# Modulation steps, casts and one transpose issued at other places of a two-layer hybrid block

## The chip, the core and the metric

One Trainium2 chip, of which the program uses one core. The metric is the device time of one execution in microseconds (us). The engines are TensorE (PE: matmuls, and PEld: its weight loads), VectorE (DVE), ScalarE (ACT), GpSimd (POOL) and SyncE (SP, which here only issues transfers). Each works through its own instructions in the order in which the program issues them, and waits on semaphores for the others.

## The reference

Two layers run over 256 latent tokens (x) and 256 context tokens (ctx), 1024 wide, in fp32. Each layer has an FFN, a mixer of three head groups (neighbourhood attention, spatial gating, retention), and a second FFN. Nine modulation vectors of 1024 (shift, scale and gate for each of the three parts) come from c for latent tokens and from c_ctx for context tokens. After the second mixer only latent tokens go on.

```python
mod_x = (jax.nn.silu(c) @ ada_w[layer] + ada_b[layer]).reshape(b, N_MOD, 1, d)
mod_c = (jax.nn.silu(c_ctx) @ ada_w[layer] + ada_b[layer]).reshape(1, N_MOD, 1, d)
x = ffn_branch(x, mod_x, 0, ...)      # h + 0.5 * gate * swiglu(rms(h) * (1 + scale) + shift)
ctx = ffn_branch(ctx, mod_c, 0, ...)
yx, yc = hybrid_mixer(...)
x = x + mod_x[:, 5] * yx
x = ffn_branch(x, mod_x, 6, ...)
if not last:
    ctx = ctx + mod_c[:, 5] * yc
    ctx = ffn_branch(ctx, mod_c, 6, ...)
return x
```

## The kernel before, in words

Tokens lie along the free axis: xT holds 8 tiles of 128 features by 512 tokens (256 latent, 256 context). Every large product is made of three matmuls on split operands: each fp32 operand is a high part (a cast to fp32r) and a low part (the rest), and high by high, high by low and low by high are added up in PSUM (L204, L206 to L208; L212 for the other layout).

**Weights.** `Stream` (L64) brings the weights in 128x1024 chunks in a fixed order. A chunk is loaded by a transfer on SP's queue into one of three `wr` buffers (L79), cast by ScalarE into `wh` (L89), and VectorE subtracts to give `wl` (L100); four buffers each. `take` hands out the next chunk and prefetches up to three more; `high_to` issues casts alone. So the low part of a chunk stands in VectorE's queue about one output tile before TensorE needs it.

**An FFN** (L625) runs in two halves. In each, `up` makes 11 gate and 11 up outputs (16 products of 512 tokens for each pair; L675 gates, L679 casts the result, L682 gives its low part), then `down` makes 8 output tiles (11 products each) and `residual` (L441) adds each to xT. In the second half the normalization of what follows is prepared: ScalarE squares each new tile (L337), VectorE adds up (L341). Where both token streams go on, the last two output tiles are done stream by stream (`split_tail`), and the first chunks of the next phase are split between them (`todo`, `hand_over`: code 1k is a cast up to chunk k, 2k a cast and low part up to chunk k). There are four FFNs: (0,0), (0,1), (1,0), (1,1). In (0,1) and (1,0) most up products use seven products for eight (`Seven`), and in (1,1) only latent tokens are left.

**The planner.** Work that is not tied to a product waits in two lists. `bg` is a list of steps; `pump` (L185) is called after every product of three matmuls, and adds `pace[0]` for 512 columns (half of it for 256); each whole one issues a step. `due` holds functions that `later` puts there with a delay in the same counts. `drain_bg` issues all that is left.

**Modulation.** `ada_steps` (L264) makes the modulation vectors on VectorE: each block of 128 outputs is one 512 KB tile `aw`, loaded by a transfer (L282), and one step per token stream multiplies it with the vector and sums (L290, whose output goes to `junk` or in place to `aw`); after 8 blocks a closing step adds the bias (L295). Vectors 5 to 8 of layer 1 need only the latent stream: one step on a tile instead of two. All 112 steps of layer 1 are spread over the FFNs by `ADA1`: for each FFN the counts in its first and second half. In (0,0) the list is 112 steps of layer 0 and then those of layer 1, at `APACE`, with five `aw` buffers on SP's queue. In (0,1) and (1,0) the steps run in the down phases, in the first half with two `aw` buffers (which the up phases use too) and in the second with four, both on POOL's queue. In (1,1) they run in the first up phase.

**The end of the last mixer.** `yt` (L1510) transposes the retention output of one pair of heads (yR, made on POOL at L1302 and L1304), ScalarE writes its high part (L1515), VectorE its low part (L1516). `proj` adds the output projection up in the order of `KORD`: features 0 to 2 are attention, 3 and 4 gating (`sg_gate`, L1379; split at L1507 and L1508), 5 to 7 retention. In layer 1 two output tiles (`NM`) are begun together while these come in.

Of the kernel before, what the change touches and what calls it, by code (L numbers as in the profile page):

```python
# [20 lines left out]
KT = D // 128  # L21
# [16 lines left out]

DIRECT = {(0, 1): (5, 0), (1, 0): (5, 0)}

ADA1 = {(0, 0): (40, 0), (0, 1): (16, 16), (1, 0): (16, 16), (1, 1): (8, 0)}

STAT, OS, FS, SPR = 3, 3.5, 2, 12

# [9 lines left out]
SUMS = 0.65  # L54
GPACE = (0.4, 0.55)
OPACE = (0.8, 0.8)
APACE = 0.345
NPACE = (0.95, 1.0)
RPACE = (1.2, 1.4)

# [74 lines left out]
def tile_hybrid_dit(ctx: ExitStack, tc: tile.TileContext, t_x, t_c, t_cb, t_ada0, t_ada, t_adab, t_nw, t_w1, t_w2,  # L135
# [12 lines left out]
    def mm_bank(name="mm"):  # L148
        return bank("mm", 4, name)
# [48 lines left out]
    def drain_bg(n=None):  # L198
        while bg and (n is None or n > 0):
            bg.pop(0)()  # L200
            if n is not None:
                n -= 1
# [16 lines left out]
    with tc.manual_schedule():  # L219
# [219 lines left out]
        def residual(l, i, m, ps, c0, streams):  # L439
            for s in streams:  # L440
                V.scalar_tensor_tensor(out=xT[:, m, s * T:s * T + T], in0=ps[:, s * T - c0:s * T - c0 + T],  # L441
                                       scalar=mod[l][:, 24 * i + 16 + m, s:s + 1], in1=xT[:, m, s * T:s * T + T],
                                       op0=ALU.mult, op1=ALU.add)
# [181 lines left out]
        def ffn(l, f, lead, norms, steps=None, tail=None):  # L625
# [7 lines left out]
            with ExitStack() as es:  # L633
# [21 lines left out]
                for half in range(2):  # L655
# [114 lines left out]
                    def down(m, wa, wb, a, b, ps):  # L770
                        for kt in range(JH):
                            w, c = (wa, kt) if kt < 6 else (wb, kt - 6)
                            product(ps[:, a:b], w, 128 * c, aTh, aTl, (slice(None), kt, slice(a, b)),
                                    kt == 0, kt == JH - 1)
# [15 lines left out]
                    for m in range(KT - 2 if split_tail else KT):  # L790
                        a, b = 0, T * len(streams)
                        wa, wb = ws.take(), ws.take(AHEAD - 1)
                        ps = mm_bank("d")
                        if ahead and m == KT - 3:
                            drain_bg()
                            seven.load(JH)
                            seven.load(JH + 1)
                            seven.add(JH)
                            seven.add(JH + 1)
                        down(m, wa, wb, a, b, ps)  # L800
                        if ahead and m >= KT - 2:
                            for s in seven.prepare(JH)[slice(0, 4) if m == KT - 2 else slice(4, 7)]:
                                s()
                        residual(l, i, m, ps, 0, streams)
                        if half == 1:
                            for s in streams:
                                if s in norms:
                                    norms[s].add(m)
                            if tail:
                                tail(m)  # L810
                    if split_tail:
                        w = [(ws.take(3), ws.take(2)), (ws.take(1), ws.take(0))]
                        for s in streams:
                            for m in (KT - 2, KT - 1):
                                ps = mm_bank("d")
                                down(m, *w[m - KT + 2], s * T, s * T + T, ps)
                                residual(l, i, m, ps, 0, (s,))
                                norms[s].add(m)
                                if s and m < KT - 1:
                                    flush_due()  # L820
                                    for f in todo(norms, steps[0]):
                                        f()
                            if s == 0:
                                later(FS, norms[0].stats)
                                later(FS + 2, norms[0].begin)
                                drain_bg()
                            else:
                                hand_over(norms, steps[1])
# [37 lines left out]
        def mixer(l, norms):  # L866
            last = l == L - 1
            ctx_out = not last
            with ExitStack() as es:
# [631 lines left out]


                yh, yl = hTh, hTl
                KORD = (0, 1, 2, 5, 6, 7, 3, 4)

                def split(src, dst):
                    S.copy(out=yh[dst], in_=src)  # L1507
# [10 lines left out]

                def proj(m, w, ps, a, b, kts=KORD):
                    for kt in kts:  # L1520
                        hh, hl = (na["oT"][:, 0], na["oT"][:, 1]) if kt < 3 else (yh, yl)
                        product(ps[:, a:b], w, 128 * kt, hh, hl, (slice(None), kt, slice(a, b)),
                                kt == KORD[0], kt == KORD[-1])

# [6 lines left out]
                for m in range(nm):  # L1531
                    if m < 3:
                        yt(m + 5)
                    proj(m, w[m], ps[m], 0, n, KORD[0:3])
                for m in range(nm, 3):
                    yt(m + 5)
                for kt in KORD[3:6]:
                    for m in range(nm):
                        proj(m, w[m], ps[m], 0, n, (kt,))
                drain_bg()  # L1540

                def finish(m, ps, ahead=AHEAD):
                    residual(l, 1, m, ps, 0, streams)
# [6 lines left out]
                            norms[0].raw(k)  # L1550

                for m in range(nm):
                    proj(m, w[m], ps[m], 0, n, KORD[6:8])
                    finish(m, ps[m], min(m + 5 - nm, AHEAD))
                for m in range(nm, KT - 3 if ctx_out else KT):
                    w = ws.take(0)
# [290 lines left out]
```

## Time and profile before

| | |
|---|---|
| time, 3 runs | 1810.83 us median (1810.07 to 1811.4) |
| profiled execution | 1812.95 us; span of the core 1811.2 us |
| mean granted TensorE clock | 0.997 |
| PE busy | 1778.7 us (98%), 11520 matmuls |
| DVE busy | 1300.8 us (72%) |
| ACT busy | 724.8 us (40%) |
| POOL busy | 260.8 us (14%) |
| HBM read | 287.64 MB |

Times in the rows are microseconds from the start of the span. A busy share is an average over stages; which engine is waited for is read stage by stage. Matmuls are pipelined: a 512-column product is shown about 0.39 us long while the next starts 0.23 us after it, a 256-column one 0.28 us long with the next after 0.12 us.

### The profile page before, as it was taken

How to read it: one execution, taken by the hardware profiler on the slowest of the kernel's cores; microseconds unless marked ns; L12 is line 12 of the kernel's file. 1: busy time of each engine (PE TensorE's matmuls, PEld its weight loads, DVE VectorE, ACT ScalarE, POOL GpSimd, SP SyncE). 2: the span in 40 equal slices, each digit the busy share in tenths (PEclk: the TensorE clock that was granted, in tenths of full speed). 3: DMA queues.
4: the chain of work that ended last, by engine and by line, in shares of the span. 5: the costliest groups of instructions: out<-in, count | busy, mean ns of one | idle time of the engine just before them, and what ended most of it. 6: DMA issues, size and time to landing. Idle time of an engine off the chain costs nothing. (4 is left out here: it accounts for less than half of the span.)

```text
span 1811.2 us, 29366 instructions
## 1 busy us (share of the span) xinstructions
PE 1778.7 (98%) x11520; PEld 1550.2 (86%) x11520; DVE 1300.8 (72%) x2200; ACT 724.8 (40%) x1203; POOL 260.8 (14%) x307
## 2 busy tenths in 40 slices
PE   7999999999999999999999999999999999999999
PEld 5788888888668989898999898979998867899998
DVE  5789988976455566788588877776887745668665
ACT  3422222225544234452344244513542555354443
POOL 0000000002114310120222002113311104310000
PEclk9999999999999999999999999999999999999999
DMA  8656765634211122656675526567666422356654
GB/s 316 236 190 217 252 212 189 212 124 149 87 64 47 47 74 67 174 147 188 179 183 158 164 86 179 153 210 199 169 188 222 146 88 76 106 192 200 200 179 148
DMA packets 103610, 290.60 MB, mean 160 GB/s; under 512 B 12080, under 2 KB 18864, under 8 KB 103344
## 3 DMA queue, kind: packets, MB, share of 16 engines
q1 hardware_dynamic: 86192, 243.64, 41.0%
q0 software_dynamic: 17280, 45.10, 10.8%
q8 instruction: 90, 1.47, 0.3%
q14 instruction: 48, 0.39, 0.1%
HBM read 287.64 MB, written 1.05 MB: 159 GB/s over the span
## 5 line engine op out<-in xcount | busy, mean ns | idle before, releaser
L100 DVE TENSOR_TENSOR wl<-wr,wh 128x1024 fp32r<-128x1024 f32 (+2 forms) x308 | 327.0, 1087 | 112.3 <-ACT wh L89 110.9
L89 ACT CAST wh<-wr 128x1024 fp32r<-128x1024 f32 (+2 forms) x308 | 279.9, 934 | 182.2 <-PE d L207 90.5
L208 PE MATMUL d<-aTh,wl 128*128 128x512 f32 (+1 forms) x770 | 269.6, 350 | 2.0 <-DVE wl L100 2.0
L206 PE MATMUL d<-aTh,wh 128*128 128x512 f32 (+1 forms) x770 | 269.9, 351 | 1.1 <-ACT wh L89 1.1
L207 PE MATMUL d<-aTl,wh 128*128 128x512 f32 (+1 forms) x770 | 269.2, 350 | 0.0
L208 PEld LDWEIGHTS d<-aTh,wl 128*128 128x128 f32 x770 | 145.3, 189 | 24.4 <-DVE wl L100 3.2
L206 PEld LDWEIGHTS d<-aTh,wh 128*128 128x128 f32 x770 | 145.2, 189 | 22.5 <-ACT wh L89 1.3
L290 DVE CUSTOM_DVE_ANT_0 aw<-aw,cb 128x1024 f32<-128x1024 f32 x128 | 155.6, 1223 | 11.5 <-DMA aw<-in_ada_dram 8.9
L207 PEld LDWEIGHTS d<-aTl,wh 128*128 128x128 f32 x770 | 145.3, 189 | 21.1
L206 PE MATMUL g<-hTh,wh 128*128 128x512 f32 (+2 forms) x464 | 158.1, 341 | 3.0 <-ACT hTh L383 1.4
L208 PE MATMUL g<-hTh,wl 128*128 128x512 f32 (+2 forms) x464 | 156.9, 338 | 2.0 <-DVE wl L100 1.9
L207 PE MATMUL g<-hTl,wh 128*128 128x512 f32 (+2 forms) x464 | 157.1, 339 | 1.3 <-DVE hTl L366 1.1
L208 PE MATMUL u<-hTh,wl 128*128 128x512 f32 (+2 forms) x464 | 156.6, 337 | 0.4 <-DVE wl L100 0.4
L206 PE MATMUL u<-hTh,wh 128*128 128x512 f32 (+2 forms) x464 | 156.1, 336 | 0.0
L207 PE MATMUL u<-hTl,wh 128*128 128x512 f32 (+2 forms) x464 | 156.0, 336 | 0.0
L214 PE MATMUL nat<-wh,hTh 128*128 128x512 f32 (+2 forms) x384 | 136.3, 355 | 0.0
L216 PE MATMUL nat<-wh,hTl 128*128 128x512 f32 (+2 forms) x384 | 127.9, 333 | 0.4 <-DVE hTl L366 0.4
L215 PE MATMUL nat<-wl,hTh 128*128 128x512 f32 (+2 forms) x384 | 127.7, 333 | 0.0
L290 DVE CUSTOM_DVE_ANT_0 junk<-aw,cb 128x1024 f32<-128x1024 f32 x96 | 117.0, 1219 | 4.5 <-DMA aw<-in_ada_dram 4.1
L582 PE MATMUL p<-hTh,wl 128*128 128x256 f32 x408 | 116.2, 285 | 0.6
L582 PE MATMUL p<-th,wl 128*128 128x256 f32 x408 | 114.8, 281 | 0.6 <-DVE wl L551 0.5
L581 PE MATMUL p<-hTl,wh 128*128 128x256 f32 x408 | 114.6, 281 | 0.0
(262 smaller groups left out, 4044.5 us busy)
## 6 DMA issues: line engine op xcount, KB each, us to landing
wr<-in_w_dram SPq DMA_DIRECT2D x142, 512.0 KB, 4.4
aw<-in_ada_dram SPq DMA_DIRECT2D x92, 512.0 KB, 5.1
wr<-in_wi_dram SPq DMA_DIRECT2D x56, 512.0 KB, 3.6
aw<-in_ada_dram POOLq DMA_DIRECT2D x52, 512.0 KB, 4.8
wr<-in_w_dram SPq DMA_DIRECT2D x64, 384.0 KB, 3.8
wr<-in_w_dram SPq DMA_DIRECT2D x64, 320.0 KB, 3.0
q<-in_w_dram SPq DMA_DIRECT2D x68, 256.0 KB, 3.8
q<-in_w_dram POOLq DMA_DIRECT2D x68, 256.0 KB, 5.3
```

The lines of the kernel that those rows point to most:

```text
L89: self.nc.scalar.copy(out=h[:, :n], in_=self.raw[i][:, :n])
L100: self.nc.vector.tensor_tensor(out=lo[:, :n], in0=t[:, :n], in1=h[:, :n].bitcast(F32), op=ALU.subtract)
L206: PE.matmul(out=ps, lhsT=wh[:, col:col + 128], rhs=hh[rhs_sl], start=start, stop=False)
L207: PE.matmul(out=ps, lhsT=wh[:, col:col + 128], rhs=hl[rhs_sl], start=False, stop=False)
L208: PE.matmul(out=ps, lhsT=wl[:, col:col + 128], rhs=hh[rhs_sl], start=False, stop=stop)
L214: PE.matmul(out=ps, lhsT=hh[lhs_sl], rhs=wh[:, wc], start=start, stop=False)
L215: PE.matmul(out=ps, lhsT=hh[lhs_sl], rhs=wl[:, wc], start=False, stop=False)
L216: PE.matmul(out=ps, lhsT=hl[lhs_sl], rhs=wh[:, wc], start=False, stop=stop)
L290: V.tensor_tensor_reduce(out=junk, in0=t, in1=cb[:, s], scale=1.0, scalar=0.0, op0=ALU.mult, op1=ALU.add, accum_out=mod[l][:, 8 * r + b, s ...
L581: PE.matmul(out=ps, lhsT=wh[:, cw], rhs=tl, start=False, stop=False)
L582: PE.matmul(out=ps, lhsT=wl[:, cw], rhs=th, start=False, stop=n == 3)
```

## The change

Five edits. The constants: eight more steps of layer 1 in (0,0), none in (1,1), and a pace of 0.38 instead of 0.345 in (0,0). Since the steps are taken from one list in order, the four places between keep their counts (16 each) and get later vectors. In the second half of each FFN with `split_tail`, the casts of the last output tile's two chunks are issued before the residual of the sixth tile. In the last tiles' second stream, the cast and the low part of the next phase's first chunk are put into the due list at 3.1 and 4.1 counts, ahead of the residual of the seventh tile. In the last layer's mixer, the projection's order takes the gating features before the last retention pair, and that pair's transpose is issued after them.

```diff
-ADA1 = {(0, 0): (40, 0), (0, 1): (16, 16), (1, 0): (16, 16), (1, 1): (8, 0)}
+ADA1 = {(0, 0): (48, 0), (0, 1): (16, 16), (1, 0): (16, 16), (1, 1): (0, 0)}
...
-APACE = 0.345
+APACE = 0.38
...
+                        if split_tail and m == KT - 3:
+                            ws.high_to(ws.n_take + 4)
                         residual(l, i, m, ps, 0, streams)
...
                                 ps = mm_bank("d")
+                                if s and m < KT - 1:
+
+                                    for n, f in enumerate(todo(norms, (11, 21))):
+                                        later(3.1 + n, f)
                                 down(m, *w[m - KT + 2], s * T, s * T + T, ps)
...
-                KORD = (0, 1, 2, 5, 6, 7, 3, 4)
+                KORD = (0, 1, 2, 5, 6, 3, 4, 7) if last else (0, 1, 2, 5, 6, 7, 3, 4)
...
-                for m in range(nm, 3):
+                for m in range(nm, 2 if last else 3):
                     yt(m + 5)
-                for kt in KORD[3:6]:
+                for kt in KORD[3:7 if last else 6]:
                     for m in range(nm):
                         proj(m, w[m], ps[m], 0, n, (kt,))
                 drain_bg()
+                if last:
+                    yt(7)
...
                 for m in range(nm):
-                    proj(m, w[m], ps[m], 0, n, KORD[6:8])
+                    proj(m, w[m], ps[m], 0, n, KORD[7 if last else 6:])
                     finish(m, ps[m], min(m + 5 - nm, AHEAD))
```

## Rows read from the trace of the kernel before

**Rows 1.** Part 1 of the page: busy time, share, instructions.
```profile
PE 1778.7 (98%) x11520; PEld 1550.2 (86%) x11520; DVE 1300.8 (72%) x2200; ACT 724.8 (40%) x1203; POOL 260.8 (14%) x307
```
**Rows 2.** TensorE's waits, 387 to 400 us: total, times, longest (us).
```profile
PE d L206 <- ACT wh L89: 1.1, 1, 1.1
PE d L208 <- DVE wl L100: 0.5, 1, 0.5
```
**Rows 3.** Busy time, one stretch: length, PE, PEld, DVE, ACT, POOL, PEclk, DMA.
```profile
393.30:396.80 3.50, 3.50 (x19) 3.50 (x19) 2.12 (x5) 0.42 (x1) 0.00 (x0) 0.52 0.86 269
```
**Rows 4.** VectorE's groups, 57 to 387 us: busy us, mean ns, idle before.
```profile
L290 DVE CUSTOM_DVE_ANT_0 junk<-aw,cb 128x1024 f32<-128x1024 f32 x75 | 91.5, 1219 | 4.5 <-DMA aw<-in_ada_dram 4.1 <-ACT cb L1718 0.4
L290 DVE CUSTOM_DVE_ANT_0 aw<-aw,cb 128x1024 f32<-128x1024 f32 x74 | 90.5, 1223 | 2.0
...
L682 DVE TENSOR_TENSOR aTl<-sg,aTh 128x512 fp32r<-128x512 f32 x22 | 15.2, 692 | 15.1 <-ACT aTh L679 15.1
L675 DVE TENSOR_TENSOR sg<-sg,u 128x512 f32<-128x512 f32 x22 | 15.0, 681 | 3.4 <-PE u L208 3.4
...
L441 DVE SCALAR_TENSOR_TENSOR xT<-d,mod,xT 128x256 f32<-128x256 f32 x26 | 11.3, 477 | 1.7 <-PE d L208 1.7
```
**Rows 5.** Timeline, PE and DVE, 156 to 165 us: start, length, what.
```profile
156.10 0.40 PE L208 MATMUL u<-hTh,wl 128*128 128x512 f32 x1
...
160.06 0.68 DVE L675 TENSOR_TENSOR sg<-sg,u 128x512 f32<-128x512 f32 x1
...
162.16 1.69 DVE L100 TENSOR_TENSOR wl<-wr,wh 128x768 fp32r<-128x768 f32 x2
...
164.51 0.39 PE L208 MATMUL d<-aTh,wl 128*128 128x512 f32 x1
```
**Rows 6.** Timeline, PE and DVE, second half of the first FFN.
```profile
340.20 0.40 PE L208 MATMUL u<-hTh,wl 128*128 128x512 f32 x1
...
341.12 0.68 DVE L675 TENSOR_TENSOR sg<-sg,u 128x512 f32<-128x512 f32 x1
...
386.40 0.39 PE L208 MATMUL d<-aTh,wl 128*128 128x512 f32 x1
...
389.63 0.87 DVE L441 SCALAR_TENSOR_TENSOR xT<-d,mod,xT 128x256 f32<-128x256 f32 x2
```
**Rows 7.** TensorE's waits, 1048 to 1056 us.
```profile
PE g L207 <- DVE hTl L366: 0.7, 1, 0.7
PE u L208 <- DVE wl L100: 0.4, 1, 0.4
```
**Rows 8.** Timeline, POOL, DVE and PE, first down phase of the third FFN.
```profile
1198.01 0.53 POOL L282 DMA_DIRECT2D aw<-in_ada_dram  x1 [4.24 <-DVE mod L290]
...
1202.91 1.23 DVE L290 CUSTOM_DVE_ANT_0 aw<-aw,cb 128x1024 f32<-128x1024 f32 x1 [3.72 <-DMA aw<-in_ada_dram]
...
1214.91 1.23 DVE L290 CUSTOM_DVE_ANT_0 aw<-aw,cb 128x1024 f32<-128x1024 f32 x1 [2.43 <-DMA aw<-in_ada_dram]
...
1218.05 0.50 PE L208 MATMUL d<-aTh,wl 128*128 128x512 f32 x1 [0.42 <-DVE wl L100]
```
**Rows 9.** TensorE's waits, 1640 to 1690 us, last FFN.
```profile
PE g L208 <- DVE wl L100: 1.5, 2, 0.8
PE g L206 <- ACT wh L89: 1.0, 2, 0.5
PE d L208 <- DVE wl L100: 0.6, 2, 0.3
```
**Rows 10.** Timeline, DVE, PE and ACT, output projection of the last mixer.
```profile
1586.41 0.86 DVE L1516 SCALAR_TENSOR_TENSOR hTl<-yt,gnw,hTh 128x256 fp32r<-128x256 f32 x2
1587.12 0.44 PE L1513 MATMUL yt<-ident,yR 128*128 128x128 f32 x2 [2.52 <-POOL yR L1304]
...
1587.60 0.47 ACT L1515 ACTIVATE hTh<-yt,gnw 128x256 fp32r<-128x256 f32 x1 [1.40 <-PE yt L1513]
...
1588.11 0.48 DVE L1516 SCALAR_TENSOR_TENSOR hTl<-yt,gnw,hTh 128x256 fp32r<-128x256 f32 x1 [0.83 <-ACT hTh L1515]
```

## The prediction

> **What bounds the kernel now.** Read the engine shares first: TensorE is busy 98% of the span [rows 1]. So only three things can move the time: waits of TensorE, stretches at its lower clock, and new waits. Read TensorE's waits next, by stretch, and ask at each who came last. At the end of the first FFN it waits 1.1 us for a cast and 0.5 us for a low part [rows 2]; right after, the clock is at 0.52 for 3.5 us, about the lower of its two levels (1.2 against 2.4 GHz) [rows 3]. Then read the engine behind it: VectorE's groups over the first FFN, with what ended its idle time [rows 4]. Most of its time is modulation steps (149 of 1.22 us), and of its idle time only 3.4 + 1.7 us ended with TensorE's products. It is nearly full, and never the bound there: TensorE has no wait between 57 and 387 us. How much later VectorE may run before it becomes the bound is the question of this change.
>
> The profiled execution took 1812.95 us, its span 1811.2; the median of the runs shown is 1810.83. The sum below is a difference on that span and is added to the median. A wait in the rows hides 0.16 us more than it shows: a 256-column product is modelled 0.28 us long, while the next follows 0.12 us later.
>
> **Modulation steps and pace in the first FFN.** The planner counts one per three 512-column products. From the product at 156.10 to that at 164.51 [rows 5] are 36 starts, so a count is 0.70 us. The FFN has after its lead 144 counts (first half up), 88 (down), 176 (second half up), 66 (six whole down tiles). The pace goes from 0.345 to 0.38, so by the end of each stretch 5.0, 3.1, 6.2 and, until the list of 173 items runs out at count 455 (four tiles), 1.5 more steps have been issued: 15.8 x 1.22 = 19.3 us of VectorE work, with four more 512 KB loads on SP's queue (which waits for VectorE's buffers in the same order, so it brings no wait of its own).
>
> How much can hide? A step waits for no product, and the low parts of the next weights stand behind it. At 160.06 the last gating of the first half starts 3.7 us after the last up product (156.10 + 0.23); its low parts, from 162.16, are one done at about 163.0, and TensorE needs that one at 164.51 [rows 5]. So 1.5 us are spare: VectorE may be 5.2 us late there, and about as much in the down tiles; about 8 us between up tiles, which last 3.5 us longer. Stretch by stretch:
> - first half up: 3.7 + 5.0 x 1.22, less some 0.5 us of the idle time, is 9.3 us late against 5.2: some 4 us of TensorE wait;
> - down: the lag falls more slowly than before; 0.4 us, and 3.5 us late at the end;
> - second half up: before, the last gating at 341.12 is 0.7 us behind the product at 340.20 (+ 0.23) [rows 6]. Now 0.7 + 3.5 carried + 6.2 x 1.22, less the 3.4 us of idle time that ended with up products, is 8.4 late against 5 allowed: 3.4 us;
> - four down tiles: 1.5 x 1.22 more, and the growth they had before (0.7 to 2.3 us late): some 2.2 us.
> Together 10 us. After a wait as long as those 1.6 us the clock fell [rows 2, 3], and 3.5 us at half rate cost 1.7. Two such drops are likely here, but while VectorE is behind a slower TensorE mostly lets it catch up: +1. I take 11; from below nothing is charged (the lag stays in the queue), from above 14 + 3.4.
>
> **End of the first FFN.** The steps run out one and a half tiles earlier, VectorE catches up (before, the residual at 389.63 comes 3.0 us after the last product [rows 6]), and the two casts stand ahead of that residual on ScalarE. The wait goes: 1.1 + 0.5 + 2 x 0.16 = 1.9 us, and with it the 1.7 us of the clock drop: -3.6, from 0 (if the lag above is still there) to -3.7. At the other two FFN ends no product waits for these casts; cost and gain nothing, covered by the 256-column products that run meanwhile.
>
> **First cast and low part of the next phase ahead of the residual.** Three places. At 1052 us TensorE waits 0.7 + 0.4 us for a normalized tile and a low part [rows 7]; both follow the second of two low parts on VectorE, and one of these now comes a tile earlier, behind the first two scaled tiles: -1.1, from 0 to -1.4. The residual behind it is up to 1.2 us later, which the last tile's 33 products (3.9 us) hide. At the other two places at most 0.3 us either way, taken as nothing.
>
> **Modulation steps in the third FFN.** The last eight steps move forward through all FFNs. The second FFN keeps 8 loads of two steps in each half. The third FFN's first down phase had 4 loads of two steps and 8 of one (12 loads); it now has 16 of one. Its tiles have two buffers, loaded from POOL's queue. One load is issued at 1198.01, and the step on it starts at 1202.91, after 3.72 us of VectorE idle; from there to 1214.91 are four steps [rows 8], 3.0 us each. The planner issues one per 2.9 counts, 2.0 us. So each step on a tile of its own puts VectorE 1.0 us further back. Before, eight of them end in a TensorE wait of 0.42 us for a low part [rows 8]: the lag is already at its limit. Eight more add 8 x 1.0, less the first two loads that come before they are needed: 6 to 9 us, nearly all wait of TensorE since nothing is spare. What is queued behind is the residual and both low parts of every tile, then the loads of the next half, which share those buffers. I take +7; from below 0 (loads in time), from above 11. The same fall-out as above in clock: within the upper bound.
> The Trainium skill, "DMA: Bandwidth & Descriptors", section on the anatomy of a DMA on the gpsimd path, gives 2.0 us plus bytes over 436 GB/s; for 512 KB that is an estimate of 3.2 us, and with it this term would be about 1 and the sum 1814.8. The trace disagrees with it: 4.90 us from issue to step. It is the second rival.
>
> **Last FFN.** Its eight steps are gone (8 loads on POOL, one closing addition). From 1640 to 1690 us TensorE waits six times, 1.5 + 1.0 + 0.6 us [rows 9], all for casts and low parts behind those steps. With 6 x 0.16 that is 4.1 us; nothing else is late there, since the neighbouring outputs without steps have no wait. -4.0, from -3 to -4.1.
>
> **Last mixer.** The third transpose waits 2.52 us for POOL, until 1587.12 [rows 10]. Moved back, TensorE next needs the tile that VectorE finishes in the pair begun at 1586.41: the first is done at about 1586.9. So the wait is nearly as long (0.2 less), because the gating's subtraction is late too. And at its new place nothing stands between the transpose and its product: from transpose to ScalarE's copy 0.48 us, copy 0.47, VectorE's low part from 1588.11 for 0.48 [rows 10], with 0.06 to restart 1.5 us, of which transpose and first product cover 0.3: +1.2. Where the clock is low at this time anyway, part is hidden: +0.7, from -0.3 to +2.
>
> **Sum.** 11 - 3.6 - 1.1 + 7 - 4.0 + 0.7 = +10.0 us: 1820.8.
>
> **The rivals.**
> - VectorE's queue takes it all (faster): gains stay, charges don't come: -3.6 - 1.1 - 4.0 + 0.7 = -8.0, 1802.8. For it: no TensorE wait from 57 to 387 us, with VectorE 3.7 us late already. Against it: the 1.5 us to spare [rows 5] and the 0.42 us wait [rows 8]. It decides at the last gating of the first half: under 5.2 us late. 0.12.
> - The third FFN's loads come nearly in time: a step every 2.0 us needs a buffer back in 4.0, so a load in 2.7; at 3.2 a buffer turns round in 4.5, a step comes every 2.2 us, and the term is 1, not 7: +4.0, 1814.8. For it, the two loads that a buffer pair keeps under way; against it, 4.90 [rows 8]. 0.12.
> - Only the first FFN absorbs: -8.0 + 7 = -1.0, 1809.8. For it, the idle time of 15.1 us behind the copies [rows 4], if a wait for ScalarE shrinks under load; against it, those waits are in each gating's own chain. 0.09.
> - Clock drops at all four new waits cost in full, 4 x 1.7 less the 1 counted: +15.8, 1826.6. For it [rows 3]; against it, VectorE is still behind during most of these waits, and then TensorE's rate is not what counts. 0.12.
> - That the edits do nothing: the counts above come from the constants that the planner reads, so none.
>
> **How the numbers follow.** The forecast keeps 0.55; its own range is 1814 to 1828. Under 0.2% (3.6 us) this measurement can't be told from no change. Slower: 0.55 + 0.12 (clock) and most of the 0.12 of the loads, which ends at the edge: 0.73. Same: 0.09 and the rest: 0.14. Faster: 0.13. The range leaves out the absorbing case and the far ends: 1806 to 1831.
>
> **What would show it.** Right: TensorE waits for low parts at about 165 to 176 us and 350 to 362 us, VectorE's last gating of the first half 8 us late; no wait and full clock at 390 to 400; steps 3 us apart at 1180 to 1225 with a TensorE wait of 5 us or more there; no wait from 1640 to 1690; a second short wait behind the third transpose. Wrong: VectorE idle for products in the first FFN as before, or steps 2 us apart in the third.

## The result, and the profile after

The changed kernel took 1821.35 us (median of 4 runs, 1819.64 to 1825.84) against 1810.72 us (4 runs, 1810.07 to 1811.4): a ratio of 1.0055, 95% interval 1.0037 to 1.0074. It is slower by 10.6 us; the forecast was 10.0 us, 1820.8.

The profiled execution is the longest of the four (1825.84, span 1824.1), so the first question is how much of its 12.9 us of extra span is the change. Part 1 of its page answers [rows 1]: no engine has more instructions, and TensorE is busy for 5.9 us longer.

```profile
PE 1784.6 (98%) x11520; PEld 1551.5 (85%) x11520; DVE 1300.3 (71%) x2200; ACT 725.0 (40%) x1203; POOL 259.4 (14%) x303
```

Both traces hold all 11520 TensorE products, so the n-th can be laid beside the n-th. The table gives, for every kernel of this study, by how much its products fall back (+) or gain (-) against those of the kernel before between two such products (us, start of the product from the start of the span; the times in the heading are those of the kernel before).

| kernel | start-up, to 80.3 | first FFN, to 370.8 | its end, to 415.7 | mixer and second FFN, to 1021.0 | to 1181.5 | third FFN, down and up, to 1316.5 | to 1578.1 | last mixer, to 1644.3 | last FFN, to 1775.0 | to 1807.3 | sum |
|---|---|---|---|---|---|---|---|---|---|---|---|
| after | 3.47 | 7.95 | -2.21 | -0.08 | -0.21 | 8.77 | 0.00 | 1.01 | -4.71 | -0.87 | 13.11 |
| e1_old_constants | 2.77 | 0.00 | -2.27 | 3.17 | -0.21 | -1.64 | -1.61 | -0.52 | 0.01 | -0.87 | -1.17 |
| e2_constants_only | 2.03 | 8.95 | -3.11 | 0.03 | -0.20 | 8.13 | -1.63 | 0.00 | -4.71 | -0.87 | 8.62 |
| e3_pace_only | 1.87 | 8.04 | -3.67 | 1.57 | 0.37 | 0.05 | -0.02 | 0.02 | -0.06 | -0.58 | 7.60 |
| e4_two_loads | 3.04 | 9.00 | -3.29 | -0.01 | -0.20 | -3.01 | -1.59 | 1.04 | -4.71 | -0.87 | -0.59 |
| e5_third_buffer | 1.63 | 9.76 | -3.75 | 0.01 | -0.20 | -3.00 | -1.58 | 1.01 | -4.71 | -0.87 | -1.70 |
| e6_spread | 0.20 | 0.00 | -3.75 | -0.07 | -0.09 | -0.79 | -1.58 | -0.01 | -1.90 | -0.87 | -8.86 |
| e7_mixer_only | 2.55 | 0.00 | -0.04 | 0.05 | -0.06 | -0.16 | -1.61 | -0.47 | -0.01 | -0.87 | -0.62 |
| e8_second_ffn20 | 3.25 | 0.00 | -2.05 | 6.74 | 0.92 | -3.01 | -1.61 | -0.01 | -4.71 | -0.87 | -1.35 |
| e9_second_ffn22 | 0.35 | 0.00 | -3.75 | 4.34 | 3.99 | -3.03 | -1.58 | -0.05 | -4.71 | -0.87 | -5.31 |
| e10_third_ffn20 | 0.68 | 0.00 | -3.74 | 0.01 | 0.97 | 0.27 | 0.36 | 0.02 | -4.71 | -0.87 | -7.01 |
| e11_third_ffn24 | 2.43 | 0.00 | -3.73 | -0.05 | 0.13 | -0.63 | 7.99 | -0.01 | -4.71 | -0.87 | 0.56 |

Each row is one execution, and so is the one that it is set against; e6's and e9's were the shortest of their ten and eleven, so their sums show more gain than their medians do. Two columns are not the change's. The start-up varies from one execution to the next: with only the mixer edited it is 2.55 us, with 36 steps in the first FFN 0.20. And the last column is -0.87 in ten of the eleven other kernels as well, with old and new constants: there the profiled execution of before had a wait of its own (0.5 us for a low part at 1799 us). Without these two the change comes to 13.11 - 3.47 + 0.87 = 10.5 us, close to the difference of the medians, 10.6.

**First FFN.** TensorE's waits from 57 to 400 us (total, times, longest), where before there were 1.1 + 0.5 [rows 2]:

```profile
PE d L206 <- ACT aTh L679: 4.6, 2, 3.1
PE d L208 <- DVE wl L100: 0.8, 3, 0.3
PE d L207 <- DVE aTl L682: 0.5, 2, 0.2
```

The two large ones begin at 168.0 and 354.6 us, and the two waits for `aTl` follow directly behind them; the three of 0.3 us are in the down tiles, at 375, 384 and 392 us. TensorE's timeline shows the last up product of the first half and the first wait (start, length, what, idle before it and what ended it); it answers to [rows 5]:

```profile
160.48 0.40 PE L208 MATMUL u<-hTh,wl 128*128 128x512 f32 x1
...
169.63 0.49 PE L206 MATMUL d<-aTh,wh 128*128 128x512 f32 x1 [1.59 <-ACT aTh L679]
```

VectorE's and ScalarE's timelines of the same stretch say why: the last gating starts at 168.25, 7.5 us after the last up product (160.48 + 0.23), right behind a modulation step that began at 167.10, and ScalarE's cast follows it after 7.62 us with nothing else to do.

```profile
167.10 1.22 DVE L290 CUSTOM_DVE_ANT_0 junk<-aw,cb 128x1024 f32<-128x1024 f32 x1
168.25 0.08 DVE L290 DVE_READ_ACCUMULATOR2_ANT mod<- 128x1 f32 x1
168.25 0.68 DVE L675 TENSOR_TENSOR sg<-sg,u 128x512 f32<-128x512 f32 x1
169.61 0.69 DVE L682 TENSOR_TENSOR aTl<-sg,aTh 128x512 fp32r<-128x512 f32 x1 [0.68 <-ACT aTh L679]
170.34 0.96 DVE L100 TENSOR_TENSOR wl<-wr,wh 128x768 fp32r<-128x768 f32 x1
```

```profile
168.96 0.62 ACT L679 CAST aTh<-sg 128x512 fp32r<-128x512 f32 x1 [7.62 <-DVE sg L675]
```

VectorE's groups from 57 to 387 us confirm it (busy us, mean ns, idle before). The steps are 158 instead of 149, and the gating's multiplication, which waited 3.4 us for TensorE's products [rows 4], never does now: VectorE is the bound.

```profile
L290 DVE CUSTOM_DVE_ANT_0 aw<-aw,cb 128x1024 f32<-128x1024 f32 x79 | 96.6, 1223 | 2.1
L290 DVE CUSTOM_DVE_ANT_0 junk<-aw,cb 128x1024 f32<-128x1024 f32 x79 | 96.3, 1219 | 4.3 <-DMA aw<-in_ada_dram 3.9 <-ACT cb L1726 0.4
...
L675 DVE TENSOR_TENSOR sg<-sg,u 128x512 f32<-128x512 f32 x22 | 15.0, 681 | 0.0
```

Being late costs a little between the up tiles too, where the page shows no wait, because it ends inside the modelled length of the product before: at four products that take a low part it loses 0.2 to 0.35 us each, 1.1 us together (at 101, 123, 146 and 157 us in the kernel before). The second of them, with VectorE's low parts, in the kernel before (two lines) and now (two lines): the first of the two low parts, 1.2 us long, was ready 2.8 us ahead of its product, and now just ends before it.

```profile
119.38 2.36 DVE L100 TENSOR_TENSOR wl<-wr,wh 128x1024 fp32r<-128x1024 f32 x2 [0.26 <-ACT wh L89]
123.40 0.40 PE L208 MATMUL g<-hTh,wl 128*128 128x512 f32 x1
126.02 2.36 DVE L100 TENSOR_TENSOR wl<-wr,wh 128x1024 fp32r<-128x1024 f32 x2 [0.26 <-ACT wh L89]
127.30 0.50 PE L208 MATMUL g<-hTh,wl 128*128 128x512 f32 x1
```

**End of the first FFN.** No wait there, and a window at the products of [rows 3], which come about 10 us later now, shows the full clock (PEclk, the third number from the end, was 0.52):

```profile
403.50:407.00 3.50, 3.50 (x32) 3.50 (x31) 1.21 (x3) 0.42 (x1) 0.00 (x0) 1.00 0.79 247
```

**Third FFN, first down phase.** TensorE's waits from 1180 to 1245 us were 0.4 for a low part [rows 8] and another 0.5 for one at the end. Now:

```profile
PE d L208 <- DVE wl L100: 8.0, 4, 3.7
```

VectorE's modulation steps (L290) in that stretch; duration, first and last start, then what ended the idle time ahead of them. Before, 8.6 us of it ended with a load, in six places:

```profile
L290 DVE CUSTOM_DVE_ANT_0 aw<-aw,cb x16: 1214/1224/1228, 1186.5 to 1233.7; 128x1024 f32<-128x1024 f32 x16
...
its engine sat idle before it (us, times) until:
  DMA aw<-in_ada_dram: 19.3, 11
```

Sixteen steps from 1186.5 to 1233.7 are 3.15 us apart. Behind the longest wait the clock is at the lower of its two levels for 3.5 us:

```profile
1226.80:1230.30 3.50, 3.50 (x10) 2.71 (x9) 1.76 (x3) 0.00 (x0) 0.53 (x1) 0.51 0.91 303
```

**Last mixer and last FFN.** The 2.52 us wait for POOL [rows 10] is gone from the third transpose. Instead TensorE waits at two places behind the transposes: for ScalarE's copy and VectorE's low part (1.30 and 0.66 us) behind the first two, and for a copy (0.57 us) behind the third:

```profile
1603.57 0.38 PE L206 MATMUL op<-hTh,wh 128*128 128x256 f32 x1 [1.30 <-ACT hTh L1521]
...
1604.61 0.38 PE L207 MATMUL op<-hTl,wh 128*128 128x256 f32 x1 [0.66 <-DVE hTl L1522]
...
1609.94 0.38 PE L206 MATMUL op<-hTh,wh 128*128 128x256 f32 x1 [0.57 <-ACT hTh L1521]
```

In the last FFN the waits of [rows 9] are gone: TensorE is busy all through (length, PE, PEld, DVE).

```profile
1655.00:1715.00 60.00, 60.00 (x504) 60.00 (x503) 39.53 (x60) 28.05 (x40) 0.00 (x0) 1.00 0.57 175
```

### The profile page after: what moved, and what is told of

It is laid out like the page before. It is cut to its first block, busy times and chain, and to the rows that moved or that the text cites. A ratio compares the mean times of both kernels' runs of the same rounds, so it can differ in the third digit from the quotient of the medians.

```text
span 1824.1 us, 29359 instructions
## 1 busy us (share of the span) xinstructions
PE 1784.6 (98%) x11520; PEld 1551.5 (85%) x11520; DVE 1300.3 (71%) x2200; ACT 725.0 (40%) x1203; POOL 259.4 (14%) x303
## 3 DMA queue, kind: packets, MB, share of 16 engines
q0 software_dynamic: 16704, 43.00, 10.6%
## 5 line engine op out<-in xcount | busy, mean ns | idle before, releaser
L208 PEld LDWEIGHTS d<-aTh,wl 128*128 128x128 f32 x770 | 144.8, 188 | 33.7 <-DVE wl L100 12.9
L290 DVE CUSTOM_DVE_ANT_0 aw<-aw,cb 128x1024 f32<-128x1024 f32 x128 | 155.7, 1222 | 22.1 <-DMA aw<-in_ada_dram 19.6
L679 ACT CAST aTh<-sg 128x512 fp32r<-128x512 f32 x66 | 41.0, 621 | 204.4 <-DVE sg L675 178.6
L290 DVE CUSTOM_DVE_ANT_0 junk<-aw,cb 128x1024 f32<-128x1024 f32 x96 | 117.0, 1219 | 6.8 <-DMA aw<-in_ada_dram 6.4
```

Of the source, the lines that this page charges most:

```text
L208: PE.matmul(out=ps, lhsT=wl[:, col:col + 128], rhs=hh[rhs_sl], start=False, stop=stop)
L290: V.tensor_tensor_reduce(out=junk, in0=t, in1=cb[:, s], scale=1.0, scalar=0.0, op0=ALU.mult, op1=ALU.add, accum_out=mod[l][:, 8 * r + b, s ...
L679: S.copy(out=aTh[:, j], in_=sg)
```

## The experiments

In the first six, parts of the change are done alone, undone, or freed of one suspected wait; the last five put the steps elsewhere. The cast and low part ahead of the residual had no run of their own. Medians of the kernel before differ by the chip that a group of runs had (1811.8 for the first four, 1812.1, 1811.9 and 1813.1), so ratios are what counts.

### e1_old_constants: the casts and the mixer without the moved steps

```diff
 (against the changed kernel)
-ADA1 = {(0, 0): (48, 0), (0, 1): (16, 16), (1, 0): (16, 16), (1, 1): (0, 0)}
+ADA1 = {(0, 0): (40, 0), (0, 1): (16, 16), (1, 0): (16, 16), (1, 1): (8, 0)}
-APACE = 0.38
+APACE = 0.345
```

> The changed kernel with both planner constants (steps per FFN and pace) back at their old values; the casts issued ahead and the mixer's order stay. My theory: the whole loss comes from VectorE's modulation steps that were moved forward, so this is within 1 us of the kernel before: +0.9 for the mixer, and at the end of the first FFN the wait (1.6 us) stays or shrinks by the cast's 1.1 us only, because the low part still stands behind VectorE's late steps; in the third FFN's first down phase TensorE waits 1.3 us as before. 1810 to 1812. Rival (the casts ahead of the residual are what costs, by putting the residual back): 3 us or more slower than before. Rival (the casts ahead alone take the wait and the clock drop at the end of the first FFN away): -3.6 + 0.9, about 1808.

Measured: 1811.35 us (11 runs), ratio 0.9998 (0.9988 to 1.0007). The whole loss is in the two constants. The third reading was right about the place though: at the first FFN's end 2.27 us come back. TensorE's only wait from 57 to 400 us is one for the low part, and the window behind it is at full clock:

```profile
PE d L208 <- DVE wl L100: 1.2, 1, 1.2
```

```profile
395.00:398.50 3.50, 3.50 (x31) 3.50 (x32) 2.47 (x5) 0.42 (x1) 0.00 (x0) 1.00 0.71 246
```

So the casts do take the 1.1 us wait of [rows 2] away; the low part behind VectorE's steps is then late by about as much, and the gain is mainly the clock drop that did not come. The time shows none of it, because in this execution 3.17 us went elsewhere: a drop to 0.50 behind a wait of 0.7 us at 612 us that every kernel has, and that eleven of the thirteen have without a drop.

### e2_constants_only: the moved steps alone

```diff
 (against the kernel before)
-ADA1 = {(0, 0): (40, 0), (0, 1): (16, 16), (1, 0): (16, 16), (1, 1): (8, 0)}
+ADA1 = {(0, 0): (48, 0), (0, 1): (16, 16), (1, 0): (16, 16), (1, 1): (0, 0)}
-APACE = 0.345
+APACE = 0.38
```

> The kernel before with only the two planner constants changed (48 steps instead of 40 in the first FFN, none instead of 8 in the last, pace 0.38 instead of 0.345). My theory: all of the change's effect but the mixer's +0.9: first FFN +7 of TensorE waits, its tail's wait gone or below 0.5 us since the steps run out early (-3 to -3.7), third FFN's first down phase +7 to +9, last FFN -4: about 1819 to 1821. Rival (the casts take the tail's wait away, not the earlier end of the steps): the tail keeps 1.6 us of wait and the clock drop, and the time is 3.6 more, 1823 to 1824. Rival (the mixer is most of the loss): within 2 us of before.

Measured: 1823.42 us (5 runs), ratio 1.0061 (1.0046 to 1.0075), that is +11.0 us (8.3 to 13.6), as much as the whole change. The table has it part by part: 8.95, -3.11, 8.13, -4.71. The end of the first FFN gains without the casts what it gains with them (the -3.11 holds a wait of 0.6 us in a down tile; behind it 3.7 us are gained): there the constants do it, because the steps run out earlier.

### e3_pace_only: the pace alone

```diff
 (against the kernel before)
-APACE = 0.345
+APACE = 0.38
```

> The kernel before with only the pace changed, 0.345 to 0.38; the numbers of steps of each FFN stay, so the third FFN keeps 12 loads in its first down phase and the last its eight steps. My theory: the first FFN's waits at 168 and 354 us appear as in the changed kernel (5 to 7 us), the wait and clock drop at its tail go (-3.7), the third FFN and the last FFN stay as before (1.3 and 3.1 us of waits): +2 to +4, 1812.5 to 1815. Rival (the third FFN is late because of the pace, not because of the number of tiles): waits of 8 us in its first down phase here too, 1820 or more.

Measured: 1818.56 us (7 runs), ratio 1.0039 (1.0023 to 1.0055), +7.1 us (4.2 to 10): more than expected. The place is as expected: 8.04 us lost in the first FFN, all of the changed kernel's, 3.67 gained at its end, nothing in the third or the last FFN. The loss there was taken too small (5 to 7), and another 1.57 us is a clock drop near 621 us, at a place where e1 had one with the old pace. TensorE's wait in the third FFN's first down phase, where VectorE's steps were kept waiting by loads for 10.3 us (8.6 before, 19.3 in the changed kernel):

```profile
PE d L208 <- DVE wl L100: 2.0, 1, 2.0
```

2.0 us and not 8: the third FFN is late because of the number of tiles, not because of the pace. (The 2.0 us are 1.6 more than before; shorter waits behind that phase, gone in most other kernels too, bring the column back to 0.05.)

### e4_two_loads: the same VectorE work without the loads

```diff
 (against the changed kernel)
-                    t = tiles[r, b] = adap[0](nload[0])
-                    adap[2].dma_start(out=t, in_=t_ada[l, r, b])
+                    if l == 1 and r in (5, 6) and nload[0] > 1:
+                        tiles[r, b] = tiles[todo[nload[0] - 2]]
+                    else:
+                        t = tiles[r, b] = adap[0](nload[0])
+                        adap[2].dma_start(out=t, in_=t_ada[l, r, b])
```

> The changed kernel, but of the 16 modulation tiles of the third FFN's first down phase only the first two are loaded and the other 14 steps use these again: 14 loads of 512 KB are left out, so two modulation vectors of the second layer are made from the wrong matrix; VectorE's steps are all there, as many and as long. My theory (the step waits for the load into one of two buffers, 3.0 us apart where 2.0 are issued): steps about 2 us apart, TensorE's waits of 8.6 us there fall under 1.5, and the clock drop at 1227 us goes: 7 to 10 us less than the changed kernel, 1811 to 1814. Rival (the steps' own VectorE time, 1.2 us each, is what is late): waits as in the changed kernel, 1821.

Measured: 1812.83 us (11 runs), ratio 0.9999 (0.999 to 1.0008) to the kernel before, so the charge of the third FFN and more is gone. VectorE's steps are the same sixteen, with no idle time ahead of them (busy us, mean ns, idle), and TensorE is busy through the whole phase:

```profile
L293 DVE CUSTOM_DVE_ANT_0 aw<-aw,cb 128x1024 f32<-128x1024 f32 x16 | 18.8, 1219 | 0.0
```

```profile
1180.00:1245.00 65.00, 65.00 (x297) 52.97 (x297) 43.76 (x72) 16.69 (x22) 5.68 (x7) 1.00 0.45 131
```

From +8.77 to -3.01 us in that column: 11.8 us hang on the loads, none on the steps' own 1.2 us.

### e5_third_buffer: all the loads, three under way instead of two

```diff
 (against the changed kernel)
-adap[:] = (lambda i: seven.pool.tile([128, CHUNK], F32, tag="aw", name="aw", bufs=2), 2, G,
-           seven.pool)
+adap[:] = (lambda i: seven.pool.tile([128, CHUNK], F32, tag="cu", name="aw", bufs=1)
+           if l and i % 3 == 2 else
+           seven.pool.tile([128, CHUNK], F32, tag="aw", name="aw", bufs=2),
+           3 if l else 2, G, seven.pool)
```

> The changed kernel with a third buffer for the one-step modulation tiles of the third FFN's first down phase (a work tile that is free there), three loads under way instead of two; nothing is left out. My theory (each step waits for a load into one of two buffers): with three, a buffer is needed back after 6 us at the issued 2.0 us per step, and a load took 3.5 to 4.9 us with the step's 1.2 behind it, so steps come about 2.0 to 2.2 us apart instead of 3.0; VectorE's idle time for loads there falls from 19.3 us to under 10, TensorE's waits from 8.6 to under 2: 7 to 9 us less than the changed kernel, 1812 to 1815. Rival (the loads themselves are the limit, 512 KB per 3.0 us with whatever number under way, since the weights' loads share the DMA engines): steps stay 3.0 us apart, 1821.

Measured: 1811.71 us (11 runs), ratio 1.0003 (0.9994 to 1.0011). The column of the third FFN is -3.00, as if the loads were not there. TensorE has no wait from 1180 to 1245 us, and VectorE's steps:

```profile
L290 DVE CUSTOM_DVE_ANT_0 aw<-aw,cb x16: 1217/1224/1226, 1184.7 to 1219.7; 128x1024 f32<-128x1024 f32 x16
...
its engine sat idle before it (us, times) until:
  DMA aw<-in_ada_dram: 7.1, 6
```

2.3 us apart instead of 3.15, though not the 2.0 us at which they are issued: six steps still waited for a load (the median from issue to landing was 4.8 us, with two buffers 4.4). What was short was the number under way, not the rate of the DMA engines.

### e7_mixer_only: the last mixer's order alone

```diff
 (against the kernel before)
-                KORD = (0, 1, 2, 5, 6, 7, 3, 4)
+                KORD = (0, 1, 2, 5, 6, 3, 4, 7) if last else (0, 1, 2, 5, 6, 7, 3, 4)
-                for m in range(nm, 3):
+                for m in range(nm, 2 if last else 3):
-                for kt in KORD[3:6]:
+                for kt in KORD[3:7 if last else 6]:
+                if last:
+                    yt(7)
-                    proj(m, w[m], ps[m], 0, n, KORD[6:8])
+                    proj(m, w[m], ps[m], 0, n, KORD[7 if last else 6:])
```

> The kernel before with only the last mixer's new order (the last pair's transpose behind the gating). My theory: TensorE's waits between the last transposes go from 2.7 to 3.6 us, split in two places: +0.9 where the clock is full, +0 to +0.3 if it falls at about that time as before; too small for the times, 1810 to 1813. Rival (the transpose moved back takes POOL's lateness off TensorE, as its place suggests): waits fall to about 1 us, -1.7, 1809 to 1810. The start-up, the same instructions as in the kernel before, shows how far its length varies from one execution to the next: if 2 to 3.5 us, the later starts seen in the other traces are such a variation and not the change's.

Measured: 1813.86 us (10 runs), ratio 1.0006 (0.9995 to 1.0017): no difference that can be told. TensorE's waits at the transposes are those of the changed kernel shown above (1.9 us for the copies, 0.7 for the low part). Counted from product to product they are 3.6 us against 2.7 before, the +0.9 expected. But the column says -0.47: here the clock did not fall at this place. With the new order it fell in three executions (the changed kernel, e4 and e5: +1.01 to +1.04) and did not in two (e1 and e7: -0.5); with the old order it fell in all eight. On the average of the five, +0.4.

### e6_spread: fewer steps in the first FFN

```diff
 (against the kernel before)
-ADA1 = {(0, 0): (40, 0), (0, 1): (16, 16), (1, 0): (16, 16), (1, 1): (8, 0)}
+ADA1 = {(0, 0): (36, 0), (0, 1): (18, 18), (1, 0): (16, 16), (1, 1): (8, 0)}
-                    bg.extend([lambda: None] * 8 + ada_steps(1, ADA1[l, f][0]))
+                    bg.extend(ada_steps(1, ADA1[l, f][0]))
+                        if split_tail and m == KT - 3:
+                            ws.high_to(ws.n_take + 4)
```

> The kernel before with the opposite move: four steps fewer in the first FFN (36 instead of 40), two more in each half of the second (18 instead of 16), the eight of the last FFN spread over it instead of bunched behind eight empty turns, the pace at its old 0.345, the mixer's order old, the casts ahead of the residuals as in the change. My theory (VectorE's backlog is what TensorE waits for at the tail of the first FFN and in the last FFN): the tail's wait (1.3 + 0.7 us before) and the clock drop behind it go, -2.3 to -3.7; the last FFN's six waits (4.1 us) go or fall under 1, -3 to -4; the third FFN keeps 1.3: 1803 to 1807. Rival (eight steps with their own loads cost the last FFN its waits wherever they stand): only -2 to -4, 1808 to 1810. Rival (two more steps per half make the second FFN late): new waits between 700 and 1060 us, same as before or slower.

Measured: 1806.82 us (10 runs), ratio 0.9976 (0.9966 to 0.9985): 4.4 us faster than before. The first FFN's end gives -3.75, its wait and its clock drop, the two that were counted. In the last FFN five waits are left and only 1.9 us come back; the second reading was partly right there:

```profile
PE g L208 <- DVE wl L100: 1.8, 5, 0.4
```

### e8_second_ffn20 and e9_second_ffn22: the eight steps into the second FFN

```diff
 (both against e6_spread; both also with the third buffer of e5_third_buffer)
-ADA1 = {(0, 0): (36, 0), (0, 1): (18, 18), (1, 0): (16, 16), (1, 1): (8, 0)}
+ADA1 = {(0, 0): (40, 0), (0, 1): (20, 20), (1, 0): (16, 16), (1, 1): (0, 0)}   (e8)
+ADA1 = {(0, 0): (36, 0), (0, 1): (22, 22), (1, 0): (16, 16), (1, 1): (0, 0)}   (e9)
```

> The kernel before with the last FFN's eight steps moved as in the change, but into the second FFN (20 steps per half instead of 16) and not the first, which keeps 40 at the old pace; a third buffer in the third FFN's first down phase; the casts ahead of the residuals; the mixer's order old. My theory: VectorE's room is in the second FFN, whose down phases (792 to 884 us) show it busy 65.5 of 92 us; four more steps of 1.2 us there make no TensorE wait. So the first FFN gives what the casts alone gave (-2.3), the third FFN -1.5, as with the third buffer in the changed kernel, and the last FFN -4.7: 1803 to 1805. Rival (any eight steps moved forward make a wait where they land): new waits of 3 us or more in the second FFN, 1807 or more.

> As the kernel with 20 steps per half in the second FFN, but 22 there and 36 instead of 40 in the first. My theory: the first FFN gives -3.7 (no wait at its tail) instead of -2.3, if the second still takes 22 in each half: 1801 to 1804. Against it, from the second FFN's pace: 22 steps of 1.2 us in a down phase of some 32 us leave VectorE little for low parts (about 0.45 us, two a tile) and residuals; if it is late there as in the first FFN, waits of 2 to 5 us at 800 to 850 and 1000 to 1045 us, 1804 to 1809.

Measured: 1811.28 us, ratio 0.9997 (0.9986 to 1.0008), and 1811.65 us, ratio 1.0002 (0.9991 to 1.0014), 11 runs each. My theory of e8 fell: VectorE had time in the second FFN, but it had to wait for its loads into two buffers. With 16 steps in its first half there was no idle time for loads; with 20 (in the stretch from 800 to 900 us)

```profile
its engine sat idle before it (us, times) until:
  DMA aw<-in_ada_dram: 9.5, 4
```

and TensorE waited 4.1 us for low parts there, 6.74 us in that column with what followed. What the third buffer and the empty last FFN gave back (-3.0 and -4.7) went there. No run gave the second FFN a third buffer, so that the buffers are the limit there too is read from this idle time and not shown. e9 fared as its second reading had it (4.34 + 3.99 us of loss), but 2.7 us above its upper bound.

### e10_third_ffn20 and e11_third_ffn24: into the phase with four buffers

```diff
 (both against e6_spread)
-ADA1 = {(0, 0): (36, 0), (0, 1): (18, 18), (1, 0): (16, 16), (1, 1): (8, 0)}
+ADA1 = {(0, 0): (36, 0), (0, 1): (18, 18), (1, 0): (16, 20), (1, 1): (4, 0)}   (e10)
+ADA1 = {(0, 0): (36, 0), (0, 1): (18, 18), (1, 0): (16, 24), (1, 1): (0, 0)}   (e11)
```

> The kernel with the steps spread (36 in the first FFN, 18 + 18 in the second), but of the last FFN's eight steps four go into the third FFN's second down phase (20 instead of 16), where four buffers are in use and VectorE never waited for a load. My theory (room is where loads are ahead and VectorE is not full: there it was busy 33.75 of 46 us, and four more steps make it 38.6): no new wait there; of the last FFN's five waits of 0.5 us about half go: 1 to 1.5 us less than with the eight, 1805 to 1806. Rival (any step moved forward makes a wait where it lands): new waits at 1345 to 1400 us, 1807 or more.

> The same with all eight of the last FFN's steps in the third FFN's second down phase (24). The last FFN has no wait left: -2.6. In the third FFN VectorE's busy time would go from 33.75 to 43.5 of 46 us, a step per 1.65 us where a load took 4.0 to 7.0 us with four buffers (1.0 to 1.75 us per load): waits of 1 to 4 us there by my theory, 1804 to 1808. Rival (only loads matter, and four buffers are enough): no wait, 1804.

Measured: e10 1805.6 us (5 runs), ratio 0.9955 (0.9939 to 0.9972); e11 1813.99 us (11 runs), ratio 1.0007 (0.9997 to 1.0017). Four more steps fit (VectorE waited 1.1 us for one load), and the last FFN then gives its whole 4.71 us. Eight do not. VectorE's busy share of that down phase (third number) and TensorE's waits in e11:

```profile
1357.00:1403.00 46.00, 40.02 (x183) 30.95 (x182) 41.66 (x79) 10.91 (x20) 8.98 (x17) 1.00 0.82 282
```

```profile
PE d L208 <- DVE wl L100: 5.4, 5, 4.2
PE d L206 <- ACT wh L89: 0.4, 1, 0.4
```

The loss in that phase is 9.6 us (the column says 7.99, since the drop behind 1568 us, 1.6 us in the kernel before, did not come here), 1.7 of it a clock drop behind the wait of 4.2 us: over twice what I had bounded it by. Both e6 and e10 beat both kernels. In its trace e10 loses 1.0 and 1.1 us in the third FFN, at its start and in its first down phase, and 1.9 us at a clock drop that e6 did not have, and gains 2.8 in the last FFN; against their own runs of the kernel before the two intervals meet, so which of them is faster stays open.

## Why the prediction was right, step by step

- **Modulation steps and pace in the first FFN: +11 predicted, 9.4 measured** (7.95 us to 370.8, and 1.4 at two late low parts in the down tiles, which the table books to the next column). The chain was right: steps issued faster, the last gating late, TensorE behind it. By its terms: first half 4 predicted, 2.4 measured at the end of the first down tile; first down phase 0.4, measured 0; second half 3.4, measured 3.9; the four down tiles 2.2, measured 2.0; the clock +1, measured 0. The lag in the second half was 8.8 us for 8.4 predicted (the last gating at 356.25, the last up product ended at 347.42); in the first it was 7.5 for 9.3, which makes up the miss there. Part of it had been paid before: the 1.1 us between the up tiles, for which the sum has nothing. There I had taken about 8 us of room for VectorE, and the lines above show 2.8. I also named the wrong waiter: I expected the wait for the low parts behind the gating; it came at the gating's own cast, which TensorE needs at the end of the first down tile, five products before the low part. The gating takes 1.38 us from its start to TensorE's product (168.25 to 169.63), and that product was due 7.0 us after the last up product (30 products of 0.233): so the room was 5.6 us and not 5.2, and the sum hardly changed. The low part was just due too: 8.2 us after the last up product [rows 5] and the 2.2 us of wait are 171.1, and it ran from 170.34 for 0.96 us.
- **The +1 for the clock** did not come in this execution. Behind the first wait the clock fell in e2 and e3, behind the second in e2, e4 and e5. But where it fell behind the first, that place cost 3.9 us instead of 2.4 and TensorE's wait in the second half was 1.7 to 1.8 us instead of 3.1: that fits a VectorE that caught up by about as much meanwhile, as the prediction had argued. The whole FFN cost 8.1 to 9.8 us in all five executions with the new pace.
- **End of the first FFN: -3.6 predicted, -3.7 measured** (the column's -2.21 without those 1.4 us), and e3 and e6 show it bare: -3.67, -3.75. The reason was half right: with the new constants the steps' early end does it (e2, without the casts, also -3.7), and the casts alone give -2.27 (e1).
- **First cast and low part of the next phase: -1.1 predicted, nothing measured.** This step failed. TensorE's two waits are those of [rows 7] to the digit:

```profile
PE g L207 <- DVE hTl L366: 0.7, 1, 0.7
PE u L208 <- DVE wl L100: 0.4, 1, 0.4
```

The first low part does come a tile earlier, at 1057.89, but it pushes the residual behind it back to 1059.02; ScalarE's second cast stands behind that residual's square, and so the second low part, which TensorE waits for, starts at 1060.98, no earlier than before: products and low part both come 9.1 us later than in the kernel before, where the second of the pair in the first line below started at about 1051.9. I had charged the later residual to the last tile's products and not followed it to what stands behind its square on ScalarE. VectorE before, then VectorE and ScalarE now, with the idle time ahead of each:

```profile
1050.73 2.36 DVE L100 TENSOR_TENSOR wl<-wr,wh 128x1024 fp32r<-128x1024 f32 x2 [0.52 <-ACT wh L89]
```

```profile
1057.89 1.22 DVE L100 TENSOR_TENSOR wl<-wr,wh 128x1024 fp32r<-128x1024 f32 x1
1059.02 0.48 DVE L441 SCALAR_TENSOR_TENSOR xT<-d,mod,xT 128x256 f32<-128x256 f32 x1
...
1060.98 1.23 DVE L100 TENSOR_TENSOR wl<-wr,wh 128x1024 fp32r<-128x1024 f32 x1 [0.52 <-ACT wh L89]
```

```profile
1059.59 0.42 ACT L337 ACTIVATE sq<-xT 128x256 f32<-128x256 f32 x1 [1.74 <-DVE xT L441]
1059.91 1.03 ACT L89 CAST wh<-wr 128x1024 fp32r<-128x1024 f32 x1
```

- **Third FFN: +7 predicted, +8.8 measured**, of which some 1.7 is the clock drop that stood in the upper bound. The steps came 3.15 us apart for 3.0 predicted. e4 and e5 show the mechanism, not only the size: without the loads, or with a third under way, the charge is gone. The estimate by the Trainium skill, "DMA: Bandwidth & Descriptors", section on the anatomy of a DMA on the gpsimd path (3.2 us for 512 KB), stands below every load of that phase: 3.7 to 5.6 us from issue to landing.
- **Last FFN: -4.0 predicted, -4.7 measured.** The six waits went, and with them shorter ones that I had left out.
- **Last mixer: +0.7 predicted, +1.0 measured**; in the five executions with the new order, -0.5 to +1.0, by whether the clock fell there. The waits themselves are as worked out.
- **The rivals.** That VectorE absorbs it all: its condition, a lag under 5.2 us, was not met (7.5). That the loads come in time: they did not, and e5 shows what it would take. That only the first FFN absorbs: it lost 9.4 us. That the clock falls at all the new waits: it fell behind one alone, that of 3.7 us in the third FFN, and in the last mixer, where it had fallen before as well. The misses (+11 for 9.4, -1.1 for 0, +7 for 8.8) cancel to within 1 us in part by chance; each sign and place but one was right.

## What to carry to other kernels

Background work moved on an engine that is not the bound is not free where that engine carries short links of the critical engine's chain: ask how late the last such link may be, and count the backlog up to it. Before moving work to a phase with idle time, ask what feeds it: here two buffers of loads were the limit in a phase in which VectorE itself had room, and a third buffer there was worth some 10 us. And follow an instruction that is pushed back to everything that stands behind its result on the next engine, not only to its own consumer.

## What the runs showed of the hardware

- The clock is not a fixed price of a wait. Behind the same wait of 3.1 us in the second half of the first FFN, the changed kernel ran at full clock (the first line below), and e5, whose instructions are the same up to there, at half (the second, another kernel's trace):

```profile
357.60:361.00 3.40, 3.14 (x12) 2.21 (x13) 3.30 (x6) 1.35 (x2) 0.00 (x0) 1.00 0.21 41
```

```profile
357.30:360.80 3.50, 3.50 (x10) 2.73 (x9) 3.43 (x7) 0.00 (x0) 0.00 (x0) 0.50 0.55 178
```

  The drop behind a wait of 1.0 us at 1568 us (-1.6 in the table's column to 1578.1 where it is missing) came in four of thirteen executions, with the same instructions ahead of it. What decides between them was not settled here.
- The start-up, with the same instructions, took 0.2 to 3.5 us longer than in the profiled execution of before. One profiled execution of each kernel thus differs by more than most edits are worth; laying product beside product takes it out.
